# Tying a decoder layer's row transpositions on TensorE, and a plain-transfer residual for its last 352 tokens

## The chip, the cores and the metric

One NeuronCore of a Trainium2 chip runs the whole kernel. The metric is the device time of one execution in microseconds (us). A core has TensorE (PE in the profile; PEld is its weight loads), VectorE (DVE), ScalarE (ACT), GpSimd (POOL), and SyncE (SP), which here issues most of the DMA transfers. GpSimd issues the accumulating ones.

## The reference, cut to what matters

One layer of a hybrid decoder on 2048 prompt tokens and 64 sample tokens (2112 rows of 1024 features, float32):

```
h = rms_norm(x, norm_mix_pre)
mix = token_mixer(h)                       # attention, state space and short convolution, then out projection
x = x + rms_norm(mix, norm_mix_post)
h = rms_norm(x, norm_mlp_pre)
f = square(relu(h @ w_mlp_up)) @ w_mlp_down   # 1024 -> 4096 -> 1024
x = x + rms_norm(f, norm_mlp_post)
```

The outputs are the last x (`y_prompt`, `y_sample`) and the caches and states of the mixer. The change touches the last three lines.

## The kernel before, in words

The kernel is one program, written in the order in which a person would read it, and a scheduler places each engine's instructions: it simulates the engines and may pull an instruction ahead of others that were written before it, if its operands are ready. `with tc.issue_after(ins):` adds an edge: what is traced inside it, on the engine of `ins`, is placed behind `ins`.

**Output projection.** `out_proj` goes over 17 tiles of up to 128 tokens (`Tok`). For each it makes 48 matmuls into two PSUM banks (pool `psA`, name `po3`, four banks in turns), and `Tok.finish` normalises, adds x, writes the sum x2 to `y_prompt` or `y_sample` in DRAM and writes the normalised rows to a DRAM scratch, `xn_d`. During the last tiles the MLP is already begun (`mlp_ahead`): its first rows are loaded and transposed, and its first weights loaded and split.

**MLP.** 2112 rows are three blocks of 704 (`BT`), each block two halves of 352 (`HT`). Both products are done by a scheme with seven products of half-sized matrices instead of eight, so a block has seven `u` (up) and seven `d` (down) products, each of eight steps: 112 steps a block in `steps`. Each product is three matmuls with a high and a low part of both operands in a 32-bit format with reduced mantissa (`mm3`: `shi`, `slo` of the rows, `whi`, `wlo` of the weights). ScalarE casts the high part, and GpSimd (up) or VectorE (down) subtracts for the low part (`w_split`, `s_pair`). Raw weights are loaded four steps ahead (`w_load`). An up step is 24 matmuls with 352 columns, a down step 18 with 512.

**Rows of the MLP.** `Half(b, t)` is one half of a block. `Half.rows` loads three tiles (128, 128, 96 tokens) from `xn_d`; `Half.turn` transposes them, one chunk of 128 features at a time: three TensorE transpositions into a PSUM bank `pq` (two banks, pool `psT`, in the first half of block 0 `psS`), and one ScalarE copy to `q` with the norm's gain. Six halves of eight chunks make 144 transpositions. `up_sums` adds and subtracts the `q` for the seven products, on VectorE.

**Who comes when.** Side work is written as generators in `streams`. `poll()`, at the end of every step, advances each one whose due time has come; time is `PE.us`, TensorE's estimated work so far, kept by `TimedPE`. `half` emits the loads, yields 18, and then emits a chunk a step. `second_half(0)` is put in `streams` before step 0 of block 0. `next_block(b)` is put there at step 38 of the 56 down steps of the block before: first its second half, then a pause of 6, then its first half. What of it is still to come after the last down step is emitted there at once, for the next step needs it (`while (b + 1, 1) not in src: advance(...)`).

**PSUM banks.** `bank()` gives the MLP's matmuls their banks in turns, from `psS` (two), `psD`, `psD` (four). `psD` is opened on the space that `psA` leaves. `nbank` starts at 2, so the first bank is number 3, in `psS`, the second number 4, in `psD`.

**The end of a block.** `mlp_out(b, t, p)` takes one tile p of the result `y` of a half: the mean square (GpSimd, with the power for the reciprocal root in `rstd_of`), a product with it and the gain `g4`, and then an accumulating DMA issued by GpSimd, which adds the tile to x2 in `y_prompt` or `y_sample`. The very last to be written are the three tiles of the third block's first half, tokens 1408 to 1759: there ScalarE makes the product of one half of the features and VectorE that of the other (`last`).

Of the kernel before, what the change touches and what calls it, by code (L numbers as in the profile page):

```python
# [10 lines left out]
F32 = mybir.dt.float32  # L11
# [8 lines left out]
P = 128  # L20
D = 1024
# [4 lines left out]
TT = S + TS  # L26
# [17 lines left out]
HT = 352  # L44
BT = 2 * HT
# [63 lines left out]
class TimedPE:  # L109
# [5 lines left out]
    def matmul(self, out, lhsT, rhs, **kw):  # L115
        n = math.prod(rhs.shape[1:])
        self.us += n / 2400 * (1 if rhs.dtype == F32R else 4)
        return self.eng.matmul(out, lhsT, rhs, **kw)  # L118

    def transpose(self, out, in_, identity):  # L120
        self.us += math.prod(identity.shape[1:]) / 1200
        return self.eng.transpose(out, in_, identity)


class Last:
# [19 lines left out]
def hybrid_layer(ctx: ExitStack, tc: tile.TileContext, I, O, stage=9):  # L145
    nc = tc.nc
    V, A, G, PE, SP = Last(nc.vector), Last(nc.scalar), Last(nc.gpsimd), TimedPE(nc.tensor), Last(nc.sync)

    cpool = ctx.enter_context(tc.tile_pool(name="const", bufs=1))
    dpool = ctx.enter_context(tc.tile_pool(name="scratch", bufs=1, space=DRAM))  # L150
# [6 lines left out]
    tot_d = dpool.tile([TS, HB], F32, name="tot_d")  # L157
    v_d = dpool.tile([TT, 256], F32, name="v_d")
    cat_d = dpool.tile([TT, D], F32, name="cat_d")
    xn_d = dpool.tile([TT, D], F32, name="xn_d")  # L160
    o_d = [dpool.tile([S, 264], F32, name=f"o_d{n}") for n in range(3)]
    acsT_d = dpool.tile([17, 8, P], F32, name="acsT_d")
# [8 lines left out]
    def cm(k):  # L171
        o, n = C_OFF[k]
        return cst[:, o:o + n]

    ident, tri, ones, trib = cm("ident"), cm("tri"), cm("ones"), cm("trib")
# [56 lines left out]
    def psb(name, bufs):  # L232
        return tc.tile_pool(name=name, bufs=bufs, space=PSUM, reuse_waits="tile")
# [55 lines left out]
    def rstd_of(pool, ss, n, d, extra=1.0, name="rstd"):  # L289

        ms = pool.tile([P, 1], F32, name=name + "_ms", tag="ms", bufs=4)
        r = pool.tile([P, 1], F32, name=name, tag="rstd", bufs=8)
        G.tensor_scalar(ms[:n], ss[:n], extra / d, EPS, op0=ALU.mult, op1=ALU.add)
        G.tensor_tensor(r[:n], ms[:n], mhalf[:n], op=ALU.pow)
        return r
# [6 lines left out]
    def y_rows(t0, n):  # L302
        if t0 < S:
            return O["y_prompt"][0, t0:t0 + n, :]
        return O["y_sample"].rearrange("b s d -> (b s) d")[t0 - S:t0 - S + n, :]
# [24 lines left out]
    def turn(xs, c0, gain, hi, lo, pools, alloc=None):  # L330

        for k in range(KC):
            if alloc is not None:
                alloc(k)
            ps, tag = pools[k % len(pools)]
            pt = ps.tile([P, 512], F32, name=f"pt{k}", tag=tag)
            w = 0
            for xt, n in xs:
                PE.transpose(pt[:, w:w + n], xt[:n, k * P:(k + 1) * P], ident[:n, :n])
                w += n  # L340
            gv = gain[:, k:k + 1]
            A.activation(hi[k][:, c0:c0 + w], pt[:, :w], AF.Copy, scale=gv)
            V.scalar_tensor_tensor(lo[k][:, c0:c0 + w], pt[:, :w], gv,
                                   hi[k].bitcast(F32)[:, c0:c0 + w],
                                   op0=ALU.mult, op1=ALU.subtract)
            yield 0.0
# [14 lines left out]
    psS = p4.enter_context(psb("psS", 2))  # L361
# [88 lines left out]
    class Blk:  # L450
# [29 lines left out]
        def build(self):  # L480
            pools = [(psT, "tr")] * 2 + [(psS, "s")] * 2 if self.smp else [(psT, "tr")]
            yield from turn(self.xs[:4], 0, gpre, self.hi, self.lo, pools, self.alloc)
            if self.smp:
                yield from turn(self.xs[4:], 512, gpre, self.hi, self.lo, pools)
# [133 lines left out]
    def in_rest(B):  # L618
# [100 lines left out]
        def finish():  # L719
# [12 lines left out]
            if B.last:  # L732
                conv_states()

        stream(finish(), 2.5)
        B.stage = 3

# [396 lines left out]
    class Tok:  # L1134
# [47 lines left out]
        def turn(self):  # L1182
            self.hi, self.lo = self.alloc()
            yield from turn([(self.ct, self.n)], 0, vec[:, V_CAT:], self.hi, self.lo, [(psT, "tr")])
# [12 lines left out]
        def square(self, hf):  # L1197
            n = self.n
            jk = epool.tile([P, 512], BF16, name="jk3", bufs=1)
            A.activation(jk[:n], self.ps[hf][:n], AF.Square, accum_out=self.ss2[:n, hf:hf + 1])  # L1200

        def finish(self):
            t, n = self.t, self.n
            ss = epool.tile([P, 1], F32, name="ss3", bufs=3)
            G.tensor_add(ss[:n], self.ss2[:n, 0:1], self.ss2[:n, 1:2])
            r = rstd_of(epool, ss, n, D)
            x2 = epool.tile([P, D], F32, name="x2t", tag="x2t")
            for hf in range(2):
                cs = slice(512 * hf, 512 * hf + 512)
                V.scalar_tensor_tensor(x2[:n, cs], self.ps[hf][:n], r[:n], gpost[:n, cs],  # L1210
                                       op0=ALU.mult, op1=ALU.mult)
            G.tensor_add(x2[:n], x2[:n], self.xt[:n])

            SP.dma_start(y_rows(t, n), x2[:n])
            sm = epool.tile([P, 2], F32, name="ssm", bufs=2)
            for hf in range(2):
                jk = epool.tile([P, 512], BF16, name="jk3", bufs=1)
                A.activation(jk[:n], x2[:n, 512 * hf:512 * hf + 512], AF.Square, accum_out=sm[:n, hf:hf + 1])
            G.tensor_add(sm[:n, 0:1], sm[:n, 0:1], sm[:n, 1:2])
            r = rstd_of(epool, sm[:, 0:1], n, D)  # L1220
            V.tensor_scalar(self.xt[:n], x2[:n], r[:n], None, op0=ALU.mult)
            SP.dma_start(xn_d[t:t + n, :], self.xt[:n])
# [350 lines left out]
    TP = [(0, P), (P, P), (2 * P, HT - 2 * P)]  # L1573
# [47 lines left out]
    class Half:  # L1621
# [13 lines left out]
        def turn(self, ps, tag):  # L1635

            self.q = [], []
            for k in range(KC):
                pt = ps.tile([P, 512], F32, name=f"pq{k}", tag=tag)
                for xt, a, n in self.xs:  # L1640
                    PE.transpose(pt[:, a:a + n], xt[:n, k * P:(k + 1) * P], ident[:n, :n])
                q = (r4 if self.t == 0 else v4).tile([P, HT], F32, name="q", tag="f")
                A.activation(q, pt[:, :HT], AF.Copy, scale=vec[:, V_MLP + k:V_MLP + k + 1])
                self.q[k // 4].append(q)
                yield 1.0
# [32 lines left out]
    psD = p4.enter_context(psb("ps4D", 4))  # L1678
# [5 lines left out]
    nbank = [2]  # L1684

    def bank():
        nbank[0] += 1
        ps, tag = ((psS, "s"), (psD, "pd"), (psD, "pd"))[nbank[0] % 3]
        return ps.tile([P, 512], F32, name="pm", tag=tag)

    XT = [(epool, "xres"), (epool, "x2t")]
# [136 lines left out]
    def mlp_out(b, t, p, last=False):  # L1828

        a, n = TP[p]  # L1830
        t0 = BT * b + HT * (t - 1) + a
        y, ss = Y.pop((t, p)), SS.pop((t, p))
        G.tensor_add(ss[:n, 0:1], ss[:n, 0:1], ss[:n, 1:2])
        r = rstd_of(e4, ss[:, 0:1], n, D)
        for d in range(2):
            cs = slice(512 * d, 512 * d + 512)
            o = y[:n, cs]
            if last and d == 0:
                A.activation(o, o, AF.Copy, scale=r[:n])
            else:  # L1840
                with tc.issue_after(V.last):
                    V.scalar_tensor_tensor(o, o, r[:n], g4[:n, cs], op0=ALU.mult, op1=ALU.mult)
        for t1, t2 in ((t0, min(t0 + n, S)), (max(t0, S), t0 + n)):
            if t1 < t2:
                G.dma_start(y_rows(t1, t2 - t1), y[t1 - t0:t2 - t0], accum_op=ALU.add)
# [23 lines left out]
    @contextmanager  # L1869
    def in_order():  # L1870

        with tc.issue_after(V.last), tc.issue_after(A.last), tc.issue_after(G.last):
            yield

    late = []

    nsplit = [1]
# [2 lines left out]
    for at, (kind, b, i, jj) in enumerate(steps):  # L1880
# [21 lines left out]
        if kind == "u":  # L1902
            hi, lo = wts.pop(at)
            s = up_s[b, i]
            for j2 in range(2):
                ps = bank()
# [4 lines left out]
        else:  # L1911
# [3 lines left out]
            for j2 in range(2):  # L1915
                j = 2 * jj + j2
                s = down_s.pop((b, i, j))
# [19 lines left out]
        if kind == "d":  # L1937
            end, last = jj == NJ // 2 - 1, b == TT // BT - 1
            if i == 2 and end and last:
                for p in range(len(TP)):  # L1940
                    o = Y[1, p][:TP[p][1], :512]
                    V.tensor_mul(o, o, g4[:TP[p][1], :512])
            if i == 3 and not end and 2 <= jj < 2 + len(TP):
                with in_order():
                    mlp_out(b, 2, jj - 2)
            if i == 3 and end:
                def finish(p, b=b, last=last):
                    square(1, p, 2)
                    mlp_out(b, 1, p, last)
                for p in range(len(TP)):  # L1950
                    if last:
                        finish(p)
                    else:
                        late.append(lambda p=p, f=finish: f(p))
# [46 lines left out]
```

## Time and profile before

| What | us |
|---|---|
| median of 3 runs (lowest, highest) | 2748.93 (2741.23, 2752.26) |
| profiled execution, its own time | 2754.54 |
| its span, first to last instruction | 2752.8 |
| TensorE busy | 2578.7 (94%) |
| VectorE busy | 1510.2 (55%) |
| ScalarE busy | 1332.3 (48%) |
| GpSimd busy | 1086.8 (39%) |

The granted clock of TensorE has a mean of 0.973. The span less TensorE's busy time, 174 us, is what waits and the two ends hold. The views that follow name an instruction by its line, engine and operation, with the tiles it writes and reads (`pm<-slo,whi` is a matmul of the MLP, `pq<-cst,xt` a transposition of its rows); in brackets stands the time that its engine sat idle before it, and what ended that. As many operations go through a few helpers, their line is often the helper's (L118 a matmul, L122 a transposition, L137 the other engines and DMAs).

### The profile page before, as it was taken

How to read it: one execution, taken by the hardware profiler on the slowest of the kernel's cores; microseconds unless marked ns; L12 is line 12 of the kernel's file. 1: busy time of each engine (PE TensorE's matmuls, PEld its weight loads, DVE VectorE, ACT ScalarE, POOL GpSimd, SP SyncE). 2: the span in 40 equal slices, each digit the busy share in tenths (PEclk: the TensorE clock that was granted, in tenths of full speed). 3: DMA queues.
4: the chain of work that ended last, by engine and by line, in shares of the span. 5: the costliest groups of instructions: out<-in, count | busy, mean ns of one | idle time of the engine just before them, and what ended most of it. 6: DMA issues, size and time to landing. Idle time of an engine off the chain costs nothing. (4 is left out here: it accounts for less than half of the span.)

```text
span 2752.8 us, 40740 instructions
## 1 busy us (share of the span) xinstructions
PE 2578.7 (94%) x14329; PEld 2179.7 (79%) x14329; DVE 1510.2 (55%) x2994; ACT 1332.3 (48%) x2785; POOL 1086.8 (39%) x1008
## 2 busy tenths in 40 slices
PE   6999898989999978999899999999999999999997
PEld 6998776877887855666799977789987779998775
DVE  4646537454455465454154457655546865445775
ACT  4534334435446323434456644554764555385453
POOL 4545435343354444434566400066620017661002
PEclk9999999999999998999999999999999999999999
DMA  6877987766677549989776566575534356543344
GB/s 200 238 188 218 266 239 213 191 184 196 177 212 208 136 130 297 297 260 287 234 221 179 169 192 199 162 224 169 168 124 154 126 176 203 174 162 130 123 153 96
DMA packets 426260, 528.26 MB, mean 192 GB/s; under 512 B 65482, under 2 KB 326130, under 8 KB 421448
## 3 DMA queue, kind: packets, MB, share of 16 engines
q1 hardware_dynamic: 411352, 483.45, 55.2%
q0 software_dynamic: 14704, 42.21, 9.5%
q8 instruction: 113, 1.85, 0.3%
q14 instruction: 91, 0.75, 0.1%
HBM read 447.90 MB, written 178.19 MB: 227 GB/s over the span
## 5 line engine op out<-in xcount | busy, mean ns | idle before, releaser
L137 POOL TENSOR_TENSOR wlo<-wraw,whi 128x512 fp32r<-128x512 f32 (+2 forms) x359 | 676.5, 1903 | 506.1 <-ACT whi L137 463.3
L137 ACT CAST whi<-wraw 128x1024 fp32r<-128x1024 f32 (+2 forms) x528 | 468.8, 891 | 401.5 <-PE pm L118 281.5
L118 PE MATMUL pm<-slo,whi 128*128 128x352 f32 x1344 | 433.2, 324 | 7.9 <-ACT whi L137 5.8
L118 PE MATMUL pm<-shi,wlo 128*128 128x352 f32 x1344 | 430.5, 326 | 5.8 <-POOL wlo L137 5.6
L118 PE MATMUL pm<-shi,whi 128*128 128x352 f32 x1344 | 435.4, 324 | 0.0
L118 PE MATMUL pm<-wlo,shi 128*128 128x512 f32 (+1 forms) x1008 | 399.0, 396 | 6.8 <-DVE wlo L137 3.9
L118 PE MATMUL pm<-whi,shi 128*128 128x512 f32 (+1 forms) x1008 | 396.0, 393 | 0.0
L118 PE MATMUL pm<-whi,slo 128*128 128x512 f32 (+1 forms) x1008 | 335.0, 396 | 3.0 <-DVE slo L137 2.5
L137 DVE TENSOR_TENSOR wlo<-wraw,whi 128x1024 fp32r<-128x1024 f32 (+1 forms) x169 | 206.2, 1220 | 192.0 <-ACT whi L137 188.8
L118 PE MATMUL pj<-lo,whi 128*128 128x512 f32 (+1 forms) x720 | 270.9, 377 | 4.9 <-ACT xr L137 2.3
L118 PEld LDWEIGHTS pm<-slo,whi 128*128 128x128 f32 x1344 | 253.6, 189 | 9.8 <-ACT whi L137 6.5
L118 PE MATMUL pj<-hi,whi 128*128 128x512 f32 (+1 forms) x720 | 261.0, 363 | 0.0
L118 PE MATMUL pj<-hi,wlo 128*128 128x512 f32 (+1 forms) x720 | 260.0, 361 | 0.0
L118 PEld LDWEIGHTS pm<-shi,wlo 128*128 128x128 f32 x1344 | 252.6, 189 | 8.5 <-POOL wlo L137 8.4
L118 PEld LDWEIGHTS pm<-shi,whi 128*128 128x128 f32 x1344 | 253.5, 189 | 0.1
L137 DVE TENSOR_TENSOR x<-pm,x 128x352 f32<-128x352 f32 x240 | 122.7, 520 | 218.2 <-PE pm L118 218.0
L118 PEld LDWEIGHTS pm<-wlo,shi 128*128 128x128 f32 (+1 forms) x1008 | 180.7, 179 | 66.3 <-ACT shi L137 12.6
L118 PEld LDWEIGHTS pm<-whi,slo 128*128 128x128 f32 (+1 forms) x1008 | 178.3, 179 | 62.1 <-DVE slo L137 12.5
L118 PEld LDWEIGHTS pm<-whi,shi 128*128 128x128 f32 (+1 forms) x1008 | 180.5, 179 | 50.3
L137 ACT CAST shi<-x 128x352 fp32r<-128x352 f32 x288 | 137.0, 484 | 152.7 <-DVE x L137 102.6
L137 ACT ACTIVATE x<-x 128x352 f32<-128x352 f32 x384 | 183.5, 495 | 46.8 <-DVE x L137 42.2
L137 POOL TENSOR_TENSOR ssf<-ssf 128x1 f32<-128x1 f32 (+1 forms) x18 | 13.8, 769 | 486.7 <-ACT jkf L137 486.6
(323 smaller groups left out, 4744.1 us busy)
## 6 DMA issues: line engine op xcount, KB each, us to landing
wraw<-in_w_in SPq DMA_DIRECT2D x192, 256.0 KB
wraw<-u_d SPq DMA_DIRECT2D x96, 512.0 KB
wraw<-d_d SPq DMA_DIRECT2D x96, 512.0 KB
wraw<-in_w_mlp_up SPq DMA_DIRECT2D x72, 512.0 KB
wraw<-in_w_mlp_down SPq DMA_DIRECT2D x72, 512.0 KB
u_d<-in_w_mlp_up POOLq DMA_DIRECT2D x64, 256.0 KB, 5.8
d_d<-in_w_mlp_down POOLq DMA_DIRECT2D x64, 256.0 KB, 7.0
out_s_k<-in_cache_attn_k SPq DMA_DIRECT2D x8, 2040.0 KB
```

The source lines that it names most:

```text
L118: return self.eng.matmul(out, lhsT, rhs, **kw)
L137: out = f(*args, **kw)
```

## The change

Four things are edited.

1. `TimedPE` keeps the last instruction that it emitted, and `Half.turn` puts the three transpositions of each chunk behind it.
2. The MLP's second bank (number 4) comes from `psS` instead of `psD`.
3. `Tok.finish` writes the rows 1408 to 1791 of x2 a second time, to a new DRAM scratch `xe_d`. At the end of the third block's second down product these rows are loaded to `xe`, three tiles in the buffers that the MLP's rows had, with SP's queue order kept.
4. For the last three tiles, `mlp_out` adds `xe` on VectorE in two halves of 512 features, and SP writes each half with a plain DMA. GpSimd's accumulating DMAs for these tiles are gone. The earlier tiles keep theirs.

```diff
     def matmul(self, out, lhsT, rhs, **kw):
...
-        return self.eng.matmul(out, lhsT, rhs, **kw)
+        out = self.eng.matmul(out, lhsT, rhs, **kw)
+        self.last = out.ins
+        return out
 
     def transpose(self, out, in_, identity):
         self.us += math.prod(identity.shape[1:]) / 1200
-        return self.eng.transpose(out, in_, identity)
+        out = self.eng.transpose(out, in_, identity)
+        self.last = out.ins
+        return out
...
+    t0e = TT - BT
+    xe_d = dpool.tile([3 * P, D], F32, name="xe_d")
...
             SP.dma_start(y_rows(t, n), x2[:n])
+            if t0e <= t < t0e + HT:
+                SP.dma_start(xe_d[t - t0e:t - t0e + n, :], x2[:n])
...
                 pt = ps.tile([P, 512], F32, name=f"pq{k}", tag=tag)
-                for xt, a, n in self.xs:
-                    PE.transpose(pt[:, a:a + n], xt[:n, k * P:(k + 1) * P], ident[:n, :n])
+
+                with tc.issue_after(PE.last):
+                    for xt, a, n in self.xs:
+                        PE.transpose(pt[:, a:a + n], xt[:n, k * P:(k + 1) * P], ident[:n, :n])
...
         nbank[0] += 1
-        ps, tag = ((psS, "s"), (psD, "pd"), (psD, "pd"))[nbank[0] % 3]
+        ps, tag = (psS, "s") if nbank[0] == 4 else ((psS, "s"), (psD, "pd"), (psD, "pd"))[nbank[0] % 3]
...
+        if last:
+
+            for d in range(2):
+                cs = slice(512 * d, 512 * d + 512)
+                V.tensor_add(y[:n, cs], y[:n, cs], xe[p][:n, cs])
+                SP.dma_start(y_rows(t0, n)[:, cs], y[:n, cs])
+            return
         for t1, t2 in ((t0, min(t0 + n, S)), (max(t0, S), t0 + n)):
             if t1 < t2:
                 G.dma_start(y_rows(t1, t2 - t1), y[t1 - t0:t2 - t0], accum_op=ALU.add)
...
+    xe = []
...
             if i == 2 and end and last:
-                for p in range(len(TP)):
+                for p, (a, n) in enumerate(TP):
+                    pool, tag = XT[p % 2]
+                    xe.append(pool.tile([P, D], F32, name="xe", tag=tag))
+                    with tc.issue_after(SP.last):
+                        SP.dma_start(xe[p][:n], xe_d[a:a + n, :])
                     o = Y[1, p][:TP[p][1], :512]
                     V.tensor_mul(o, o, g4[:TP[p][1], :512])
```

## The prediction

> **What bounds the kernel now.** I read the busy shares first, then TensorE's waits in the half of the span that the change touches, then the order of time around the longest wait, around a block boundary and at the end.
>
> ```profile
> PE 2578.7 (94%) x14329; PEld 2179.7 (79%) x14329; DVE 1510.2 (55%) x2994; ACT 1332.3 (48%) x2785; POOL 1086.8 (39%) x1008
> PE pq L122 <- DMA xt<-xn_d: 9.9, 3, 7.3
> PE pm L118 <- ACT whi L137: 5.8, 2, 3.3
> PE pm L118 <- POOL wlo L137: 5.6, 7, 1.5
> PE pm L118 <- DVE slo L137: 4.7, 6, 1.4
> PE pm L118 <- DVE wlo L137: 3.9, 3, 1.8
> PE pm L118 <- ACT shi L137: 2.6, 8, 0.6
> ```
>
> The first row is the page's; the others are TensorE's waits from 1250 us to the end, with the sum, the number and the longest. TensorE (PE) is busy 94% of the span, and from 1250 us on these waits sum to 32.5 us. The matmuls are the floor; nothing in the change removes one. What can go is part of these waits and what follows the last matmul. The largest wait is the transpositions' (pq, in `Half.turn`) for rows still being loaded, 9.9 us in three places, and 7.3 of it is one hole:
>
> ```profile
> 1328.51 0.63 PE L118 MATMUL po<-wohi,clo 128*64 128x512 f32 x2
> 1336.48 0.69 PE L122 MATMUL pq<-cst,xt 128*128 128x128 f32 x2 [7.34 <-DMA xt<-xn_d]
> 1336.82 0.64 PE L118 MATMUL pm<-slo,whi 128*128 128x352 f32 x1
> 1340.48 0.34 PE L118 MATMUL pm<-slo,whi 128*128 128x352 f32 x1
> 1344.00 0.43 PE L118 MATMUL pm<-shi,wlo 128*128 128x352 f32 x1 [0.35 <-POOL wlo L137]
> 1328.00:1336.40 8.40, 1.14 (x5) 0.40 (x3) 1.40 (x2) 2.33 (x7) 3.26 (x4) 0.84 0.97 272
> 1336.40:1340.50 4.10, 4.02 (x15) 4.03 (x16) 0.74 (x1) 0.79 (x3) 0.91 (x3) 0.50 1.03 342
> ```
>
> These are TensorE in order of time (start, length, what, the wait before it), then two stretches (length, busy time of PE, PEld, DVE, ACT and POOL, granted clock, DMA share, GB/s). Output projection ends at 1329.14; two transpositions of the second half's rows stand ahead of MLP matmuls whose operands are ready; the rows are being loaded while the DMAs are 0.97 busy. Then the clock is granted at 0.50 for the next 4.1 us: the twelve matmuls from 1336.82 to 1340.48 take 3.66 us, where a pitch of 0.16 us (1803.05 to 1803.21 below) would make 1.92.
>
> **The change part by part.** *(a) The second half's transpositions.* In program order they come after seven steps of block 0: the rows are issued at the first poll, then 18 units of TensorE's own count pass, at 24 x 352 / 2400 = 3.52 a step. Before, the scheduler was free to pull them up; now each feature chunk stands behind the last matmul emitted, some 27 us after the projection, when the rows (there at 1336.48) have long landed. So the 7.34 us go, the 1.74 of slow matmuls, 0.2 of two slow transpositions (0.69, against 0.44 for two at 1281.64 below), and the 0.35: 9.6 us in all. What is late next? The first MLP bank was computed early in both versions; bank 4 moves to the pool psS, so it can follow the projection at once, and ends at 1329.14 + 1.92 = 1331.06. Bank 5 is the first in pool psD, whose banks the projection held:
>
> ```profile
> 1331.83 1.40 DVE L137 SCALAR_TENSOR_TENSOR x2t<-po,rstd,gpost 64x512 f32<-64x512 f32 x2 [4.72 <-POOL rstd L137]
> 1333.31 2.33 POOL L137 TENSOR_TENSOR x2t<-x2t,xres 64x1024 f32<-64x1024 f32 x1 [1.51 <-DVE x2t L137]
> 1340.43 1.05 ACT L137 CAST whi<-wraw 128x1024 fp32r<-128x1024 f32 x1 [3.28 <-PE pm L118]
> 1341.56 2.39 POOL L137 TENSOR_TENSOR wlo<-wraw,whi 128x1024 fp32r<-128x1024 f32 x1 [3.25 <-ACT whi L137]
> ```
>
> The last reader of the projection's banks is VectorE at 1331.83 to 1333.23, one bank at 1332.5: bank 5 waits up to 1.5 us. The third step's weights are split when bank 4 frees their buffers (1340.43 to 1343.95, 3.5 us), so now from 1331.06 to 1334.6, or behind the 2.33 us addition on POOL to about 1338; step 2 is due at 1332.5 + 3.84 = 1336.4, so 0 to 1.5 us. I take 1.5 and 1: 9.6 - 2.5 = **7 us gained** (bounds 9.6 and 4, the lower one where the shorter hole halves the clock for as long as the row shows). The sums of rows (VectorE, from step 14) need the eighth chunk right after step 13; ScalarE's copy of a chunk lies inside the three sums ahead of it, so nothing is charged.
>
> *(b) The first half's and the other waits of pq.* 9.9 - 7.3 leaves 2.6 us (2.0 at 1281.64, 0.5 in block 0). The first half's transpositions are only 12 units behind their load, about when the rows land, so the tie need not remove the 2.0. Against it stand three new transfers into xe_d (512 KB each) in the busiest stretch of the DMAs:
>
> ```profile
> 1281.64 0.44 PE L122 MATMUL pq<-cst,xt 128*128 128x128 f32 x2 [2.01 <-DMA xt<-xn_d]
> 1282.24 2.73 SPq L137 DMA_DIRECT2D out_y_prompt<-x2t  x1
> 1250.00:1300.00 50.00, 47.99 (x247) 35.21 (x246) 25.31 (x61) 25.45 (x73) 22.27 (x33) 0.97 0.97 291
> ```
>
> At 291 GB/s 1.5 MB are 5.4 us of DMA time, and one such output issue already sits 2.73 us on SP's queue, ahead of the next tokens' loads. TensorE is 96% busy there, so most is covered. I take **0.5 us gained** (2.6 gained to 3 lost, if loads for the projection slip with the queue).
>
> *(c) The block boundaries; a cost.* For blocks 1 and 2 the first half's 24 transpositions are emitted when the block before has emitted its last matmul, for its load comes two steps earlier and is forced there. Before, they were pulled up some 50 us:
>
> ```profile
> 1753.62 0.77 PE L122 MATMUL pq<-cst,xt 128*128 128x128 f32 x6
> 1754.31 0.99 ACT L137 ACTIVATE q<-pq,vec 128x352 f32<-128x352 f32 x2
> 1799.68 2.03 ACT L137 CAST shi<-q 128x352 fp32r<-128x352 f32 x5
> 1799.81 2.27 DVE L137 TENSOR_TENSOR slo<-x,shi 128x352 fp32r<-128x352 f32 x1 [0.61 <-ACT shi L137]
> 1802.00 1.82 DVE L137 TENSOR_TENSOR slo<-q,shi 128x352 fp32r<-128x352 f32 x4
> 1802.35 0.86 PE L118 MATMUL pm<-whi,slo 128*128 128x512 f32 x3
> 1803.05 0.33 PE L118 MATMUL pm<-slo,whi 128*128 128x352 f32 x1
> 1803.21 0.32 PE L118 MATMUL pm<-shi,whi 128*128 128x352 f32 x1
> ```
>
> Two chunks are six transpositions (0.77 us) and two ScalarE copies (0.99); 1802.35 is the end of block 0's down phase and 1803.05 the first matmul of block 1, without a gap, since shi and slo were made from 1799.68 on. Tied, the chain starts only at the boundary: transposition, copy, shi, slo, matmul. Two PSUM buffers let copies and transpositions overlap. To the fourth chunk's slo: 0.69 to the first copy, four copies (2.0), four shi (1.6), one slo (0.5) = 4.8 us; that chunk's three matmuls (0.48) and the second bank (1.92) end the step at 7.2. The work in that time is 3.1 of transpositions, which are moved and not added, and 3.84 of matmuls, 6.9 in all. So a hole of 0.3 if all interleaves; if ScalarE does all eight copies first and the chunks go pair by pair (1.68 each, 1754.31 + 0.99 - 1753.62), 6.7 + 1.0 + 3.84 = 11.5, a hole of 4.6. ScalarE and VectorE carry weight casts and the last `y` sums too. I take 1.5, nearer the first, as a shi needs only its own copy: **3 us lost** over two boundaries (0.6 to 9.2). The second halves' transpositions come one chunk a step (2 x 24 of them), each behind a step, with rows loaded long before: nothing.
>
> The 7.34 us hole was followed by a clock of 0.50 for 4.1 us, so 2 us lost. [...]
>
> *(d) The end.* The accumulating transfers of POOL are replaced by an addition on VectorE and six plain transfers on SP.
>
> ```profile
> 2734.43 0.84 PE L118 MATMUL pm<-whi,slo 128*128 128x512 f32 x3
> 2737.54 0.75 DVE L137 SCALAR_TENSOR_TENSOR y<-y,rstd,gpost 128x512 f32<-128x512 f32 x1 [0.80 <-POOL rstd L137]
> 2739.14 0.75 DVE L137 SCALAR_TENSOR_TENSOR y<-y,rstd,gpost 128x512 f32<-128x512 f32 x1 [0.85 <-POOL rstd L137]
> 2741.20 1.17 POOL L137 DMA_DIRECT2D out_y_prompt<-y  x1
> 2741.55 0.75 DVE L137 SCALAR_TENSOR_TENSOR y<-y,rstd,gpost 96x512 f32<-96x512 f32 x1 [1.66 <-POOL rstd L137]
> 2742.84 0.82 POOL L137 DMA_DIRECT2D out_y_prompt<-y  x1 [0.47 <-issue]
> 2565.49 1.28 DVE L137 TENSOR_TENSOR y<-y,gpost 128x512 f32<-128x512 f32 x2
> out_y_prompt<-y POOLq DMA_DIRECT2D x1, 384.0 KB, 7.6
> out_y_sample<-y POOLq DMA_DIRECT2D x1, 256.0 KB, 4.2
> out_y_prompt<-y POOLq DMA_DIRECT2D x1, 128.0 KB, 2.8
> ```
>
> The last matmuls end at 2735.3. The last transfer leaves at 2742.84 and lands 7.6 us later, 2750.4; the span ends 2.4 after. Now VectorE does, per tile, one product (0.75) and two additions of 128x512 (0.64 each, as the pair at 2565.49): 2.0 us, three tiles in order from 2737.54, 2743.6 with 0.1 for the first wait on ScalarE. POOL no longer issues between its rstd steps, so the third rstd comes earlier than 2741.5 and is hidden. The last plain transfer is 192 KB; landings of 2.8 (128 KB) and 4.2 (256 KB) bracket it, and I take 3.3: 2746.9 instead of 2750.4, **3.5 us gained**. If the six transfers run no faster than the accumulating ones it is 1, if small ones land at once 5. [...] The loads of xe (three on SP at the end of the second down product of block 2, 1.4 MB) have some 170 us to land, and weights are loaded four steps ahead: nothing; without that cover, 5 us.
>
> Sum: -7 - 0.5 + 3 - 3.5 = **-8 us**. The profiled execution took 2754.54 us (span 2752.8), so 2746.5 for it; it stands 5.6 us above the median of 2748.93 shown, so 2741 for the median.
>
> **Rivals.** *Everything covered:* bank 5 finds a free psD bank, the boundaries interleave, the rows of the first half are there, small transfers land at once: -9.6 - 2.6 + 0.6 - 5 = -16.6 us, 2732, just beyond 0.5%. For it speaks that the scheduler filled the boundary without a gap before; against it the order bank 4, bank 5 at 1332.5. *The hole only moves:* TensorE still idles after the projection, now for the bank's reader at 1333.2 and the weights' split on POOL, the clock falls, and (a) is 4 while (b) loses 2 and (c) is 5: -4 + 2 + 5 - 3.5 = -0.5, 2748. The 2.33 us addition ahead on POOL speaks for it. *Slower, by the boundary chain:* each slo of a boundary takes 2.27 us, as at 1799.81 beside POOL's weight split, and all eight copies go first: 6.7 + 0.4 + 4 x 2.27 + 3.84 - 6.9 = 13 us a boundary, 26 - 11 = +15, 2764. From 5.5 us a boundary nothing is gained, from 12.4 it is slower by over 0.5%. Against it: the four slo at 1802.00 took 1.82 together. *It does nothing:* the ties could leave the first order only where the matmuls had no earlier place; in (a) seven steps lie between, so this holds for (b) alone.
>
> **How the numbers follow.** 0.5% (13.7 us) is about what a measurement of this kernel can tell from no change; three runs before lay within 11 us. Forecast 0.50, everything covered 0.20, hole moves 0.18, boundary chain 0.12. Faster by over 0.5% takes most of the second and a little of the first: 0.22; slower most of the last: 0.09; within: 0.69. The range 2731 to 2753 leaves out the boundary chain and little else; it takes in the spread of the runs.
>
> **What would show it.** (a) No wait of pq at the projection's end, the next wait under 3 us, clock near 1. (b) The wait at about 1281 between 0 and 4 us. (c) Six-fold pq groups right at the two boundaries, the first matmul of the next block 2 to 5 us behind the last one, a new wait on shi or slo. (d) Last matmul to span end 14 us instead of 17.5 (2735.3 to 2752.8). Wrong: a boundary hole above 5 us, or a hole of 5 us left at the projection's end.

## The result, and the profile after

| | us |
|---|---|
| changed kernel, median of 22 runs | 2762.48 |
| kernel before, median of 22 runs beside it | 2746.69 |
| ratio, 95% interval | 1.0055 [1.0043, 1.0066] |
| profiled execution of the changed kernel, its span | 2748.0 |
| the same before | 2752.8 |

The change makes the kernel 15 us slower by the ratio; 8 us less was forecast. The ratio leaves out one of the 22 runs of the changed kernel, which took 3143.91 us at a granted clock of 0.749. The two spans stand the other way round, since the traced execution of the changed kernel, at 2749.72 us, is the second fastest of its 22. Up to the output projection the engines carry out the same instructions in the same order, and yet this front takes 989.6 us in the trace before and 975.3 in the trace after, so the traces are read stage by stage from the projection on. The stages are worked out from the first and last matmul of each kind: `out` the projection, `u0` to `d2` the up and down products of the three blocks, `tail` from the last matmul to the end of the span.

```
           front    out     u0     d0     u1     d1     u2     d2   tail   u0 to tail
before     989.6  339.5  229.0  245.1  223.1  244.3  224.4  240.3   17.5   1423.6
after      975.3  338.6  241.8  240.0  231.9  240.2  226.8  239.4   13.9   1434.0
```

The loss is in u0, 12.8 us; the tail gives 3.6 back. The boundaries lie in d0 to u2 together: 936.9 before, 938.9 after. From the projection's end to the end of the span that is 10.4 us; the other 5 of the ratio's 15 can't be placed from one trace of each.

The busy row of the page, and then TensorE's waits from 1250 us to the end (sum, number, longest), the two views that opened the prediction:

```profile
PE 2575.3 (94%) x14329; PEld 2179.5 (79%) x14329; DVE 1517.8 (55%) x3000; ACT 1332.4 (48%) x2785; POOL 1079.7 (39%) x1005
```

```profile
PE pm L118 <- ACT whi L141: 18.0, 10, 4.5
PE pm L118 <- DVE slo L141: 6.5, 6, 3.0
PE pm L118 <- POOL wlo L141: 5.5, 10, 1.0
...
PE pq L124 <- ACT q L141: 2.4, 6, 0.5
```

The transpositions' 9.9 us of waits for rows are gone, and matmuls wait 18.0 us for the high parts of the weights (`whi`) where they waited 5.8. TensorE in order of time, from the projection's end at 1313.95 (start, length, what, the wait before it): first the rows with a wait up to 1341.63, then one step and the start of the next with their transpositions and ScalarE's cast, and last the final transpositions:

```profile
1314.88 0.43 PE L118 MATMUL pm<-slo,whi 128*128 128x352 f32 x1 [0.93 <-ACT x L141]
1317.78 0.43 PE L118 MATMUL pm<-slo,whi 128*128 128x352 f32 x1 [0.70 <-DVE x2t L141]
1338.01 0.43 PE L118 MATMUL pm<-slo,whi 128*128 128x352 f32 x1 [2.62 <-ACT whi L141]
1341.63 0.66 PE L118 MATMUL pm<-slo,whi 128*128 128x352 f32 x1 [2.71 <-ACT whi L141]
...
1361.55 0.32 PE L118 MATMUL pm<-shi,wlo 128*128 128x352 f32 x1
1361.71 0.46 PE L124 MATMUL pq<-cst,xt 128*128 128x128 f32 x3
1361.95 1.05 ACT L141 CAST whi<-wraw 128x1024 fp32r<-128x1024 f32 x1
1363.05 0.43 PE L118 MATMUL pm<-slo,whi 128*128 128x352 f32 x1 [0.88 <-ACT whi L141]
1364.38 0.43 PE L118 MATMUL pm<-shi,wlo 128*128 128x352 f32 x1 [0.42 <-POOL wlo L141]
1367.71 0.46 PE L124 MATMUL pq<-cst,xt 128*128 128x128 f32 x3
...
1385.70 0.46 PE L124 MATMUL pq<-cst,xt 128*128 128x128 f32 x3
```

And in stretches (length, busy time of PE, PEld, DVE, ACT and POOL, granted clock, DMA share, GB/s):

```profile
1335.00:1342.00 7.00, 1.68 (x8) 1.10 (x7) 0.00 (x0) 5.04 (x7) 4.90 (x3) 0.78 0.62 185
1342.00:1350.00 8.00, 8.00 (x40) 8.00 (x40) 0.00 (x0) 0.94 (x2) 2.12 (x1) 0.77 0.57 186
1350.00:1392.00 42.00, 34.27 (x204) 31.07 (x203) 12.35 (x16) 23.04 (x42) 19.47 (x10) 1.00 0.65 206
```

The 7.3 us hole is gone, as forecast. Instead six steps from 1355.79 on last 6.0 us. Read one: its last matmul starts at 1361.55 and ends at 1361.87; at 1361.95 ScalarE begins to cast the next step's `whi`. That is the time at which the step before gives its buffers back, so the reading is that the cast waits for a buffer, and TensorE for the cast (0.88) and GpSimd's low part (0.42); the experiments put it to the test. From 1350 on the clock is 1.00 and the DMAs are 0.65 busy, so neither holds these steps up.

Who took the buffers stands in the code. `idle_y` lets the weight splits of up steps, from the block's second product (step 8) on, use pool `y4`, which has six buffers (`sb("y4", 6, "left")`), and `halves[b, t] = Half(b, t, XT if b else [(y4, "y")])` puts block 0's second rows into the same pool. Three row tiles leave three buffers: one pair of `whi` and `wlo`, and an odd one. The odd one gave no head start: GpSimd's `wlo` begins at 1361.94, `whi` at 1361.95, both behind the step. Why the odd buffer wasn't used is not shown. Before, the last of these transpositions ran at 1361.42, 32 us after the projection; tied, one chunk a step, it runs at 1385.70, 72 us after.

### The profile page after: what moved, and what is told of

It is laid out like the page before. It is cut to its first block, busy times and chain, and to the rows that moved or that the text cites. A ratio compares the mean times of both kernels' runs of the same rounds, so it can differ in the third digit from the quotient of the medians.

```text
span 2748.0 us, 40739 instructions
## 1 busy us (share of the span) xinstructions
PE 2575.3 (94%) x14329; PEld 2179.5 (79%) x14329; DVE 1517.8 (55%) x3000; ACT 1332.4 (48%) x2785; POOL 1079.7 (39%) x1005
## 5 line engine op out<-in xcount | busy, mean ns | idle before, releaser
L141 POOL TENSOR_TENSOR wlo<-wraw,whi 128x512 fp32r<-128x512 f32 (+2 forms) x359 | 669.8, 1881 | 523.8 <-ACT whi L141 449.8
```

Source lines behind the costliest of these rows:

```text
L141: out = f(*args, **kw)
```

## The experiments

Three theories were put against each other. *Buffers*: the rows held longer leave the weight splits one pair. *Boundary*: the transpositions that now stand at a block's start cost time. *Loads*: the raw weights come late right after the projection. Ratios are to the kernel before, on the same chip. u0 and the other stages are read from the one profiled execution of each run.

**The two halves of the change.** First the residual alone, edits 3 and 4:

```diff
-                with tc.issue_after(PE.last):
-                    for xt, a, n in self.xs:
-                        PE.transpose(pt[:, a:a + n], xt[:n, k * P:(k + 1) * P], ident[:n, :n])
+                for xt, a, n in self.xs:
+                    PE.transpose(pt[:, a:a + n], xt[:n, k * P:(k + 1) * P], ident[:n, :n])
...
-        ps, tag = (psS, "s") if nbank[0] == 4 else ((psS, "s"), (psD, "pd"), (psD, "pd"))[nbank[0] % 3]
+        ps, tag = ((psS, "s"), (psD, "pd"), (psD, "pd"))[nbank[0] % 3]
```

> The residual edit alone (second copy of the rows, their load, VectorE additions, plain transfers); transpositions and bank as before. All theories: last matmul to span end 13.9 us as in the changed kernel, not 17.5, and block 0's up products take 229 us from the projection's last matmul, as before; so about 3.5 us faster than before (ratio 0.9987). If the three extra transfers cost something in the projection, 0 to 2 us slower than before instead.

Then the ties and the bank alone, edits 1 and 2:

```diff
-            if t0e <= t < t0e + HT:
-                SP.dma_start(xe_d[t - t0e:t - t0e + n, :], x2[:n])
...
-        if last:
-
-            for d in range(2):
-                cs = slice(512 * d, 512 * d + 512)
-                V.tensor_add(y[:n, cs], y[:n, cs], xe[p][:n, cs])
-                SP.dma_start(y_rows(t0, n)[:, cs], y[:n, cs])
-            return
...
-                        SP.dma_start(xe[p][:n], xe_d[a:a + n, :])
```

> The ties and the bank alone, without the residual edit. Theory 'buffers' (the rows of block 0's second half lie in pool y4, are held until step 13, and leave the weight splits from step 8 on without a spare buffer) and theory 'loads' (raw weights come too late once TensorE starts earlier) both: block 0's up products about 242 us from the projection's last matmul, 18 to 19 us slower than before in all (1.0068). Theory 'boundary' (the chain at the starts of blocks 1 and 2): also slower, but with 229 us in block 0.

Measured: the residual alone 0.9977 [0.9962, 0.9991], tail 13.5 us and u0 226.9; the ties alone 1.0069 [1.0051, 1.0087], tail 16.6 and u0 246.8. All of the loss belongs to the ties and the bank; the residual part is a small gain by itself. Two sizes were missed: with the residual alone u0 is 226.9 where 229 was expected, its wait for rows being 5.41 us; with the ties alone it is 246.8 where 242 was expected, and there the first hole for raw weights is 6.05 us, where the changed kernel has 2.62.

**Is it the pool?** The whole change, with the second rows of block 0 in the buffers that the other halves use:

```diff
-        h = halves[b, t] = Half(b, t, XT if b else [(y4, "y")])
+        h = halves[b, t] = Half(b, t, XT)
```

> The changed kernel with the rows of block 0's second half in the two pools that the later halves use (xres, x2t) and not in y4; ties kept. 'Buffers': the steps with transpositions from step 8 on fall from 6.0 to about 4.3 us, block 0's up products to about 230 us, 12 us faster than the changed kernel, within 0.2% of before (1.001). 'Loads': the waits of whi for raw weights stay, and the pitch of 6 us with them, no change. 'Boundary': no change.

And the whole change with that one half untied:

```diff
-                with tc.issue_after(PE.last):
+                with ExitStack() as es:
+                    if self.t0 != HT:
+                        es.enter_context(tc.issue_after(PE.last))
```

> The changed kernel with the tie taken from block 0's second half alone; the other five halves stay tied, bank 4 in psS, residual edit kept. 'Buffers': the rows leave y4 early again, so no 6 us steps; the wait of pq at the projection's end comes back (7 us); block 0's up products 229 us, 12 to 13 us faster than the changed kernel (ratio to before 1.001). 'Boundary': the loss stays, 1.0055, since both boundaries keep their ties.

(`t0` equals `HT` in the second half of block 0 alone.) Measured: 0.9992 [0.9979, 1.0005] and 0.9987 [0.9972, 1.0003], u0 226.9 and 226.8. With the half untied the wait for rows came back, at 3.48 us for the 7 expected. Bank 4 is in `psS` in both runs, so the bank isn't what makes the loss. TensorE's waits from 1310 to 1420 us with the rows elsewhere, and then, in order of time, the longest of them and the start of two transpositions:

```profile
PE pm L118 <- ACT whi L141: 4.4, 2, 4.1
PE pm L118 <- DVE slo L141: 2.1, 2, 1.6
```

```profile
1339.90 0.66 PE L118 MATMUL pm<-slo,whi 128*128 128x352 f32 x1 [4.12 <-ACT whi L141]
1361.86 0.46 PE L124 MATMUL pq<-cst,xt 128*128 128x128 f32 x3
1366.05 0.46 PE L124 MATMUL pq<-cst,xt 128*128 128x128 f32 x3
```

The same window of the changed kernel has eight waits for `whi`, 10.6 us, and six for `wlo`, 2.5. With nothing moved but three tiles, a step with a transposition is 4.2 us again (1361.86 to 1366.05) with the tie in force, and 14.9 us of u0 are back. One hole for `whi` stays, 4.1 us at 1339.90, 27 us after the projection: ScalarE waits there 2.32 us for the raw weights to land before it casts them. That is *loads*, and it takes back most of what the tie gains.

**The hold without a tie.** The kernel before, none of the change; only the row tiles are kept:

```diff
+            if at == 13:
+                for xt, _, n in halves[0, 1].xs:
+                    hold = e4.tile([P, 1], F32, name="hold", bufs=3)
+                    with tc.issue_after(A.last):
+                        A.copy(hold[:n], xt[:n, :1])
```

> The kernel before, with nothing of the change in it. The three row tiles of the second half of block 0 are only kept in their pool y4 until step 13 of the MLP: three one-column ScalarE copies, emitted there, read them. Theory 'buffers' (with the ties the three tiles are held till step 13, the weight splits from step 8 on have three buffers in place of six, and each step waits for its own matmuls to give the pair back): the steps from about +35 us after the projection to about +70 us last 6.0 us in place of 4.3, the up phase of block 0 goes from 229.0 to about 240 us, the time to 1.004 of before (1.002 to 1.006), all else as before. Theory 'ties' (the late transpositions themselves, or the order that the tie forces on TensorE, lengthen the steps): no tie is here, the up phase stays at 227 to 230 us and the time at 1.000 (0.999 to 1.002).

Measured: 1.0168 [1.0142, 1.0194], u0 248.4. TensorE in order of time, those rows that have a wait:

```profile
1368.96 0.43 PE L118 MATMUL pm<-slo,whi 128*128 128x352 f32 x1 [1.18 <-ACT whi L137]
1370.19 0.43 PE L118 MATMUL pm<-shi,wlo 128*128 128x352 f32 x1 [0.32 <-POOL wlo L137]
1374.85 0.43 PE L118 MATMUL pm<-slo,whi 128*128 128x352 f32 x1 [1.18 <-ACT whi L137]
1376.17 0.43 PE L118 MATMUL pm<-shi,wlo 128*128 128x352 f32 x1 [0.41 <-POOL wlo L137]
1380.84 0.43 PE L118 MATMUL pm<-slo,whi 128*128 128x352 f32 x1 [1.18 <-ACT whi L137]
...
1388.37 0.43 PE L118 MATMUL pm<-slo,whi 128*128 128x352 f32 x1 [1.18 <-ACT whi L137]
...
1401.88 0.43 PE L118 MATMUL pm<-slo,whi 128*128 128x352 f32 x1 [1.18 <-ACT whi L137]
1403.21 0.43 PE L118 MATMUL pm<-shi,wlo 128*128 128x352 f32 x1 [0.41 <-POOL wlo L137]
```

The same pair of waits, at steps of 5.9 to 7.5 us, from +45 us until the copies run at 1402.7 (+79). So the hold alone makes the long steps, without any tie. The size was missed, 46 us for 11: 19.4 are in u0, whose long steps are partly longer still, and 22.3 in d0, with a wait of 13.6 us for `shi`. The three copies also changed the order that the scheduler gave to other work: of GpSimd's DMA issues into `d_d` (the sums of down weights) 23 stood between +72 and +361 us and 4 between +361 and +430 in the kernel before, here 2 and 25, ahead of that wait. So what lies in d0 says nothing of the buffers.

**What makes the raw weights late?** In the changed kernel VectorE stood 8.96 us for a load, and SP's queue 4.6 us behind VectorE's `xres`. From VectorE's, then SP's and last ScalarE's order of time:

```profile
1327.34 0.43 DVE L141 TENSOR_SCALAR gpost<-gpost 128x512 f32<-128x512 f32 x1 [8.96 <-DMA gpost<-in_norm_mlp_post]
...
1328.45 0.47 SPq L141 DMA_DIRECT2D xn_d<-xres  x1
...
1329.64 0.59 SPq L141 DMA_DIRECT2D wraw<-in_w_mlp_up  x1
...
1332.20 7.69 SPq L141 DMA_DIRECT2D wraw<-in_w_mlp_up  x2
...
1335.97 1.99 ACT L141 CAST whi<-wraw 128x1024 fp32r<-128x1024 f32 x2 [5.54 <-DMA wraw<-in_w_mlp_up]
```

So that scaling of `g4` was put later, once with the rows elsewhere (run twice) and once with the change as it is:

```diff
-    V.tensor_scalar(g4[:, 512:], g4[:, 512:], -1.0, None, op0=ALU.mult)
...
+        if at == 20:
+            with tc.issue_after(V.last):
+                V.tensor_scalar(g4[:, 512:], g4[:, 512:], -1.0, None, op0=ALU.mult)
```

> The whole change with the second half's rows of block 0 in the XT buffers, and besides, VectorE's sign change of half of g4 (which waited 9.0 us for its load in the trace of the changed kernel, ahead of VectorE's other work at the start of the MLP) moved to step 20. Theory 'sign' (the late VectorE holds up the last rows of xn_d, with them SP's loads of the halves' rows, and behind these the raw weights): the hole of 4.1 us at 27 us after the projection's last matmul is under 1 us, the up phase of block 0 goes from 226.9 to about 223 us, the time to 0.9977 of before (0.9965 to 0.999). Rival 'queue' (SP stands behind its own write of xn_d, whose landing took 5.0 us, whatever VectorE does): the hole stays at 3 to 5 us, up phase 226 to 228 us, ratio 0.9992 (0.998 to 1.000).

> The whole change as it is, with only VectorE's sign change of half of g4 moved to step 20. Theory 'buffers': the steps of 6.0 us from +35 to +70 us stay, since the three row tiles are still held. By theory 'sign' the two holes of 2.6 and 2.7 us at 23 to 30 us after the projection go as well: up phase of block 0 at 237 to 238 us in place of 241.8, ratio 1.0038 (1.002 to 1.0055). By 'queue' they stay: 241 to 243 us, ratio 1.0055 (1.004 to 1.007).

Measured: 0.9984 [0.9967, 1.0001] and, again, 0.9986 [0.9972, 1.0000], with u0 225.5 in both and holes for `whi` of 0.32 and 3.07 in the first, 0.44 and 2.91 in the second; and for the sign alone 1.0044 [1.0030, 1.0059] with u0 241.8, holes of 1.50 and 2.65, and the steps of 6.0 still there. *Sign* falls as the cause: a hole of 3 us stays where under 1 was expected, though the late-sign run's u0 fits neither theory and its ratio both. In that run VectorE's row shows who else was late, and SP's queue from 1300 to 1360 us (waited for, sum, number, longest) what it stands behind:

```profile
1331.91 0.75 DVE L141 TENSOR_SCALAR xres<-x2t,rstd 64x1024 f32<-64x1024 f32 x1 [6.08 <-POOL rstd L141]
```

```profile
SPq L141 <- POOL wlo L141: 12.2, 6, 3.5
...
SPq L141 <- DMA xn_d<-xres: 6.4, 3, 4.9
```

VectorE now waits for GpSimd's `rstd`, and this row comes 10.5 us after the projection, against 10.7 in the run with the rows elsewhere and the sign in its old place: the edit hardly moved it. In the change as it is the edit brings the row from 13.7 to 10.5 us, and yet the two holes only fall from 5.33 to 4.15 in sum, with u0 as before. SP stands longest behind GpSimd's `wlo`, 7.9 us behind the transpositions, 7.1 behind GpSimd's `x2t` and 6.4 behind its own write of `xn_d`. That doesn't contradict *queue*, but it doesn't single it out; no run took any of these away, so the cause of this hole of some 3 us stays open.

**Do the boundaries cost anything?** The late-sign run with the first halves of blocks 1 and 2 untied, run twice:

```diff
-                with tc.issue_after(PE.last):
+                with ExitStack() as es:
+                    if self.t0 < BT or self.t == 1:
+                        es.enter_context(tc.issue_after(PE.last))
```

> As the run with the late sign, with the first halves' transpositions of blocks 1 and 2 left untied as in the kernel before (ties stay in block 0 and in the second halves). Theory 'boundary costs nothing': the transpositions that stand at the boundary in a clump of 15 only change places with waits of the same length, the sum of the phases from the first block's down phase to the last block's up phase moves by less than 2 us, ratio within 0.001 of the run with the late sign. Theory 'boundary' (3 us for two boundaries, as predicted): 3 us less, ratio 0.001 lower than that run.

> The run with the late sign once more, beside the next one on one chip. In the two profiles MLP and end took 1414.9 us here and 1417.0 us there, though the other run's median was 11 us lower. If the stages before the MLP, which are the same instructions in both, only vary from run to run, this run gives 0.998 of before (0.9965 to 0.9995) and the next one comes to within 0.0015 of it; if untied boundaries are worth something that the one profile missed, the next one stays 0.003 to 0.004 lower.

> The run with the first halves of blocks 1 and 2 untied once more. 'Variation': 0.997 of before (0.996 to 0.9985), within 0.0015 of the run with the late sign beside it, and the sum of the phases from the first down phase to the last up phase within 2 us of its. 'Boundary': 0.9945 again (0.993 to 0.996), 0.003 to 0.004 below the run beside it.

Measured: 0.9945 [0.9923, 0.9967] first, 0.9968 [0.9951, 0.9986] the second time, beside 0.9984 and 0.9986 with the ties on. In the traces d0 to u2 sum to 936.8 and 936.0 us untied, and to 936.1 and 936.5 tied: no difference. The medians do differ, by 0.0039 and 0.0018 (11 and 5 us), both times in favour of untied boundaries; the first is larger than either theory gave, the second near to what was called variation. A gain between nothing and these sizes stays open, and the traces don't show where it would lie. A boundary that costs the predicted 3 us isn't seen in any sum of stages, but a single trace could hide it: among the seven traces with all first halves tied, d0 to u2 sum to 935.0 to 940.3, and in three with no tie at all (the kernel before, the residual alone, and the last run below) to 936.9 to 940.2.

**Where is a tie worth having?** With ties in block 0 alone (the run before with `if self.t0 < BT`; rows elsewhere and late sign stay), and with no tie and the rows elsewhere (the residual run and `Half(b, t, XT)`; bank 4 in `psD`, the sign in its old place):

> As the run before, with ties in block 0 alone. Theory: the transpositions of the second halves of blocks 1 and 2 are not waited for with or without a tie, so up phases of 225 to 228 us in both blocks, and a ratio within 0.0015 of the run before. Rival (the ties there keep TensorE from waiting, as in block 0): an up phase 3 to 6 us longer in block 1.

> The residual part alone with the second half's rows of block 0 in the XT buffers, no tie anywhere and the sign where it was. If the tie of block 0 is worth what the wait for the rows cost (5.4 us in the residual run, 7.3 in before), this run is 3 to 5 us slower than the run with ties in block 0 alone, ratio 0.9985 (0.997 to 0.9995), with a wait for rows of 3 to 7 us in the first 30 us of the MLP. If the time that the tie saves there is only passed on to the wait for the raw weights, as in the runs so far, the two are within 0.001.

Measured: 0.9977 [0.9963, 0.9991], u0 226.2, u1 224.6, u2 222.1; and 1.0006 [0.9992, 1.0021], u0 231.5. TensorE's waits of the first 100 us of the MLP, with ties in block 0 and then with none:

```profile
PE pm L118 <- ACT whi L141: 3.5, 1, 3.5
...
PE pm L118 <- DVE x2t L141: 0.7, 1, 0.7
```

```profile
PE pq L124 <- DMA xt<-xn_d: 3.8, 1, 3.8
PE pm L118 <- DVE x2t L141: 3.5, 1, 3.5
```

With the rows elsewhere in both, u0 is 5.3 us shorter with block 0's ties, bank 4 in `psS` and the late sign (which moved the ratio by 0.0006 to 0.0011 in the runs above). The wait for rows, 3.8, is gone with the tie, and against it stands the 3.5 for raw weights; most of the wait for the bank's reader is gone with the bank, which the run without ties hasn't moved. So the wait that the tie saves is passed on nearly whole, and more of the difference is the bank's than the tie's, as far as the waits tell. The time, 8 us less, went further than the 3 to 5 expected. The ties of the second halves of blocks 1 and 2 are worth nothing, as expected; u1 and u2 came out below the 225 to 228 given.

One comparison bears on what a tie is worth at all. The residual run has no tie and leaves the rows in `y4`, and it has u0 226.9 and 0.9977. That is no worse than the whole change with the rows elsewhere (226.9 and 0.9992) or the run with block 0's ties (226.2 and 0.9977). Moving the rows without a tie cost 4.6 us of u0 (226.9 to 231.5) and 0.0029 of the ratio, and the run with block 0's ties, the bank and the late sign won that back. A gain over the residual alone is seen only in the two runs with the first halves of blocks 1 and 2 untied, 0.9945 and 0.9968, and the second lies inside the residual run's interval, 0.9962 to 0.9991.

## Why the prediction was wrong

It gave 2741 with a range of 2731 to 2753, and the time is 2762.48. By its steps:

**(a), forecast -7, measured +12.8 in u0: the step that failed is "What is late next?".** Its first half held: no wait of pq after the projection, and in its place 0.93 and 0.70 where 2.5 was allowed. But it looked for the next late thing among banks and the third weight split, within eight microseconds, and costed the later date of the transpositions (the last behind step 13 instead of step 7 or so) at nothing: "so nothing is charged". It never asked what the transposed tiles keep occupied. Six steps of 6.0 instead of 4.2 us make 10.8; the two holes for raw weights, 2.62 and 2.71, make 5.3. VectorE's `slo` behind the late sums waits 4.2 instead of 2.2, 2.0 more. The clock, at 0.78 and 0.77 from 1335 to 1350, costs 2.2: TensorE's 9.7 us of work there times 0.22 to 0.23. With the 1.6 of the two small waits that is 21.9 against the 9.6 removed, +12.3. These terms are read from one trace of each kernel. Without the hold u0 was 226.9, a gain of 2.1: of the 7 us, 4.1 went to the raw weights' hole; the step looked at the split of the third step's weights, and not at the loads of the later ones. Even the 2.1 can't be put down to the ties, since u0 is 226.9 without any tie in the residual run.

**(b), forecast -0.5.** The wait at 1281 is gone; one of 1.9 for `clo` stands in the projection. `out` is 338.6 for 339.5, so -0.9; but over the traces of all runs `out` goes from 334.4 to 342.0, the longest without the copies into `xe_d`, so neither a gain of 0.5 nor a cost of the copies can be read from it. That the number came near is luck.

**(c), forecast +3, measured +2.0 in the sum of d0 to u2, and 0.1 with the ties alone.** The chain was told as the trace has it. TensorE in order of time at block 1's start, with ScalarE's first copy, and then both boundaries as stretches:

```profile
1795.66 0.77 PE L124 MATMUL pq<-cst,xt 128*128 128x128 f32 x6
1796.16 0.55 ACT L141 ACTIVATE q<-pq,vec 128x352 f32<-128x352 f32 x1
1796.77 0.52 PE L124 MATMUL pq<-cst,xt 128*128 128x128 f32 x3 [0.34 <-ACT q L141]
1797.83 0.52 PE L124 MATMUL pq<-cst,xt 128*128 128x128 f32 x3 [0.53 <-ACT q L141]
1798.65 0.52 PE L124 MATMUL pq<-cst,xt 128*128 128x128 f32 x3 [0.31 <-ACT q L141]
1799.34 0.44 PE L118 MATMUL pm<-slo,whi 128*128 128x352 f32 x1 [0.16 <-DVE slo L141]
```

```profile
1795.60:1799.30 3.70, 2.40 (x16) 1.49 (x14) 3.70 (x6) 3.57 (x9) 3.10 (x3) 1.00 1.01 290
1799.30:1802.70 3.40, 3.36 (x12) 3.33 (x13) 2.98 (x6) 1.72 (x5) 0.76 (x2) 0.56 0.76 237
2267.70:2271.40 3.70, 2.38 (x16) 1.49 (x14) 3.70 (x6) 3.57 (x10) 3.12 (x3) 1.00 0.40 130
2271.40:2275.00 3.60, 3.58 (x23) 3.57 (x24) 3.18 (x6) 2.73 (x7) 0.85 (x3) 1.00 0.49 150
```

Waits of 1.34 us (0.34, 0.53, 0.31, 0.16), nearly the 1.5 that was taken, and the clock fell at one boundary of two. TensorE's waits in u1 and u2 show that part of this is won back in the same stages: those for `q` and `slo` are new, 1.4 us in each, but those for GpSimd's `wlo` fall from 2.7 and 2.6 us to 1.5 and 1.5, which the prediction didn't look for. What is left is less than the sums differ from trace to trace. The rival of a boundary chain of 13 us, the only one given on the slow side, is refuted; the slow side came by another way.

**(d), forecast -3.5, measured -3.6 (tail 17.5 to 13.9), by two errors that cancel.** VectorE and SP at the end, the last matmul having ended at 2734.10:

```profile
2737.88 6.69 SPq L141 DMA_DIRECT2D out_y_prompt<-y  x6
2741.53 1.29 DVE L141 TENSOR_TENSOR y<-y,xe 96x512 f32<-96x512 f32 x2 [1.19 <-ACT y L141]
2742.74 0.74 DVE L141 SCALAR_TENSOR_TENSOR y<-y,rstd,gpost 96x512 f32<-96x512 f32 x1
2743.52 0.69 DVE L141 TENSOR_TENSOR y<-y,xe 96x512 f32<-96x512 f32 x1
```

The additions end 10.1 us behind the last matmul (2744.21), not 8.3, since the third `rstd` was not hidden: VectorE waited 1.19 for ScalarE's product with it. From there to the end of the span, 2748.0, it is 3.8 us, where 5.7 (3.3 for the landing and 2.4) was taken. The two misses, +1.8 and -1.9, cancel by luck. The gain itself is firm: with the new residual the tail is 13.5 to 14.1 us in every trace, without it 16.6 to 17.5.

Forecast by these four, with (a) as it was measured, the sum is +12.8 - 0.9 + 2.0 - 3.6 = +10.3.

## What to carry to other kernels

An instruction that is moved later keeps its operands' buffers until then: for every step that is delayed, look up the pool of what it reads, count the buffers, and find who else draws from that pool in the meantime. Where a wait at a fixed lag behind another engine's last use recurs at an even pitch, look for a pool that has fallen to one pair, and try it by moving the tiles, not the instructions. Here the best version seen has the new residual, block 0's rows in the other buffers and ties that leave the first halves of blocks 1 and 2 free, at 0.9945 and 0.9968 of before; the residual alone, without any tie, is at 0.9977.

## What the runs showed of the hardware

Two boundaries with the same waits were granted different clocks: after 3.7 us in which TensorE was busy for 2.40, the clock was 0.56 for the next 3.4 us; after 3.7 us with 2.38 busy it was 1.00. The seven traces with all first halves tied have 14 such boundaries, each with 1.33 to 1.35 us of waits: in two, the first boundary of the changed kernel and of the run with the sign alone, the clock fell to 0.56 and 0.59 over the next 3.4 us, and in the other twelve it stayed at 1.00. What brings the clock down at one boundary and not at another is not shown: by the rows of the two boundaries under (c), TensorE was busy for 65% of the stretch before the 0.56 (2.40 of 3.70 us) and for 64% of the one before the 1.00 (2.38 of 3.70).

The front, the same instructions in the same order, took 975.3 us in the trace after and 989.6 in the trace before, and lay between these in the traces of all other runs. These 14 us are more than most of the edits tried here moved.
